# The opening of a two-layer trunk on one core: x first on the link, c spread from two row groups, A and B of the first tiles in steps, idle transposes in a second place, and other orders

## The chip, the cores and the metric

The kernel runs on one core of one Trainium2 chip. The metric is the device time of one launch in microseconds (us). The core has five engines that work side by side: TensorE (PE) for matrix products, VectorE (DVE) and ScalarE (ACT) for elementwise work, GpSimd (POOL), which this kernel leaves alone, and SyncE (SP), which issues most of the loads and stores. Engines wait for one another by semaphores. Each runs its own list of instructions in order, so an instruction that waits holds up all that stand behind it on its engine. Loads and stores run on 16 DMA engines, the link to memory. TensorE writes its sums into PSUM, which has eight banks of 128 x 512 numbers; everything else lies in SBUF, in 128 partitions.

## What is computed

The reference runs `DEPTH` = 2 layers over a residual stream x of 256 rows and 2048 columns. Cut to what matters:

```python
def hybrid_layer(x, c, ...):
    mod = (c @ w_ada + b_ada)[:, None, :]
    shift, scale, gate = jnp.split(mod, 3, axis=-1)
    h = rms_norm(x, g_pre) * (1 + scale) + shift
    z = h @ w_in
    u, g_pool, q, k, v, g_diff = jnp.split(z, splits, axis=-1)
    pool_out = multiscale_pool(u, w_pool, pool_scale) * jax.nn.silu(g_pool)
    q, k = apply_rope(q, cos, sin), apply_rope(k, cos, sin)
    att = rms_norm(diff_attention(q, k, v, lam), subln_g) * (1.0 - lam_init)
    diff_out = att.reshape(B, S, D_DIFF) * jax.nn.silu(g_diff)
    y = jnp.concatenate([pool_out, diff_out], axis=-1) @ w_out
    return x + (1 + gate) * rms_norm(y, g_post)
```

c is one vector of 2048 numbers, `w_ada` is 2048 x 6144, `w_in` 2048 x 6144 and `w_out` 2048 x 2048 in each layer, all in float32. Every weight is used once for 256 rows.

## The kernel before

**Tiles.** The 256 rows are two row tiles of 128 (`st` 0 and 1). The 2048 columns of x are 16 k tiles of 128, taken in pairs (`kp` 0 to 7). `w_in` has 12 column blocks of 512, named by what they hold: U 0 and 1, GP 2 and 3, Q 4 and 5, K 6 and 7, V 8 and 9, GD 10 and 11. A `Unit` is one block with one pair of k tiles: 512 KB of weights. A weight is split into a rounded part (`whi`, a copy on ACT) and a rest (`wlo`, a subtraction on DVE), and h likewise, so that three fast products make one of full precision. Only the first group of units (three blocks with the first pair) is multiplied in float32 directly from the loaded tile (`rawz`), at about twice the time per product, for which no split is needed.

**The vector c.** `w_ada` isn't multiplied on TensorE. It comes transposed, 128 output columns at a time (`nt` 0 to 47: shift, scale and gate, 16 each), in two halves `i` of 1024 (512 KB each). DVE multiplies each half with c, which stands in every partition (`cb`), and adds up along the row (`ada`, one instruction of 128 x 1024, its sum into `mod`). Behind the two halves of shift and scale, `ab` makes A (the shift with its bias) and B (the scale with bias and `g_pre`) of these k tiles by three small operations. c is loaded into one row and spread to 128 partitions by four products with a row of ones (`spread_c`), each copied from PSUM by ACT; the third and fourth copies stand behind the squares of the first row tile.

**h.** `first_squares` sums the squares of x, `rms` makes the norm's factor from them (a sum, a root on ACT, three small operations on DVE), `scaled` scales x, PE transposes it, and ACT applies A and B (`modulated`). `make_h` and `half_h` do this for the first pair in halves by row tile. `half_h` keeps its bank with the transposed x until A and B of both k tiles are made and it has issued `first(0)` and `first(1)`, the rounded parts of h. With `st` 0 it also issues `WARM` = 18 transposes of the identity on PE, whose output nobody reads.

**Banks.** `BANKS` = 4 and `ACCS` = 4. The sums of the first two blocks of the first group lie in the `accs`, those of the third in two of the four `banks` (`prepare`, `wide`; they are named accb in the trace). The other small PSUM work takes from the rest of `banks`.

**Order.** The order on every engine is made by a planner, `Flow`, when the program is built. Each part of the kernel is a `Task` that asks for one instruction after another; the planner keeps an estimate of every engine's time, and at each step gives the turn to the request that can start first, by due times (`due`). `COST`, `MB_US`, `LANDING` and `FIRST` are its prices; `SLACK` is a margin that transposes and small products get on PE behind the estimated end of what they read; `need(u, before)` is the time at which unit u will be reached, less a lead. `RATE` says how many halves of `w_ada` are counted per unit when `plan` lays out the units, and `ORDERS` which column block takes which place in the order in which a layer's blocks end. The first steps of PE's main stream (`steps`) are: the first k tile of three blocks with row tile 0, then with row tile 1, then the second k tile of three blocks with both.

**Loads.** `begin` issues c, the positions and, by `first_loads`, x, the first halves of `w_ada` and the raw weights, all on SP's queue in the order of issue. ACT's queue takes two constants: `consts` (the frequencies and an identity) and `cols` (biases and gains by column).

Of the kernel before, what the change touches and what calls it, by code (L numbers as in the profile page):

```python
# [14 lines left out]
I32 = mybir.dt.int32  # L15
# [8 lines left out]
P = 128  # L24
# [105 lines left out]
class Flow:  # L130
# [9 lines left out]
    TABLE_US = 1.29  # L140
    MB_US, LANDING, FIRST = 0.38, 2.4, 2.2
    COLD = (1.8, 4.0)

    SLACK = 1.5
    NEAR = {"tensor": 0.0, "vector": 0.1, "scalar": 0.1, "gpsimd": 0.1, "sync": 0.0}
# [65 lines left out]
    def next_of(self, k, asks):  # L211

        rows = []
        for t in asks:
            a = t.ask
            if a.dep is None:
                a.dep = self.depends(a)
            us = a.us + self.TABLE_US * bool(a.table and a.table[0] != self.table)
            due = t.due()
            slack = self.SLACK * (k == "tensor" and 0 < due < 1e8)  # L220
            rows.append((due, max(self.now[k], a.dep + slack), us, t))
        rows.sort(key=lambda r: r[:2])
# [28 lines left out]
    def turn(self, key, op, outs, ins, total, table):  # L251
# [7 lines left out]
        a.also, self.cur.also = self.cur.also, []  # L259
        a.names = {r[0] for r in a.outs + a.ins} | {r[0] for _, r in a.also}  # L260
        a.dep, a.f32 = None, key == "tensor" and op == "matmul" and ins[-1].dtype == F32
        if a.dma:
# [142 lines left out]
class Kern:  # L405
# [169 lines left out]
    def run(self):  # L575
# [10 lines left out]
        self.wps, self.G, self.nlam, self.band = [None] * DEPTH, [None] * DEPTH, None, None  # L586
        self.rope_made = False
        self.ada_tiles = {}
# [3 lines left out]
    def begin(self):  # L592
        nc, a, f = self.nc, self.a, self.f
        self.cb = self.const([P, D], "cb")
        nc.sync.dma_start(self.cb[0:1, :], a["c"])
        consts = self.const([P, HALF + P], "consts")
        nc.scalar.dma_start(consts, a["consts"])
        self.invf, self.ident = consts[:, :HALF], consts[:, HALF:]
        self.pos_i = self.const([P, NST], "posi", I32)
        nc.sync.dma_start(self.pos_i, a["positions"])  # L600
        self.cols = self.const([P, DEPTH, 89], "cols")
        nc.scalar.dma_start(self.cols, a["cols"])
        self.x = [self.const([P, D], f"x{st}_") for st in range(NST)]
# [9 lines left out]
        self.root_table()  # L613
        self.arrived, self.squared = [False] * NST, False
        f.spawn(self.first_loads, -95.0)
        f.spawn(self.spread_c, -90.0)
        for st in range(NST):
# [12 lines left out]
        for l in range(DEPTH):  # L630
            f.spawn(lambda l=l: self.load_pool_weights(l))
            for kp in range(8):
                f.spawn(lambda l=l, kp=kp: self.make_h(l, kp), self.need_h(l, kp, 4.0))

    def first_loads(self):
# [12 lines left out]
        tiles = {u: self.big.take([P, 2, NB], "raw", kind="raw") for u in us}  # L648
        x(0)
        for e in self.adas[:4]:  # L650
# [21 lines left out]

# [185 lines left out]
    def ada(self):  # L858

        v = self.nc.vector  # L860
        for e in self.adas:
# [17 lines left out]
    def ab(self, l, k0, k1):  # L879
# [26 lines left out]
    def first_squares(self, st):  # L906
# [6 lines left out]
        if st:  # L913

            f.wait(lambda: self.made[0])
            more = self.big.take([P, D // 2], "junk")
            self.nc.vector.scalar_tensor_tensor(
                more, x[:, c[1]], self.ROOT**2, x[:, c[1]], op0=ALU.mult, op1=ALU.mult, accum_out=ss[:, st, 3:4]
            )
            self.big.give(more)  # L920
# [55 lines left out]
    def half_h(self, l, kp, st, hi, lo, whole):  # L976
# [11 lines left out]
        if whole is not None and not st:  # L988

            d = self.bank()  # L990
            for i in range(self.WARM):
                nc.tensor.transpose(d[:, 0:P], self.ident, self.ident)
            self.banks.give(d)

# [24 lines left out]
        rest(0), rest(1)  # L1019
        self.used_whole(kp)  # L1020

    def used_whole(self, kp):
# [221 lines left out]
    def heads(self, l, hp):  # L1244
# [11 lines left out]
        for h in range(2):  # L1256
# [183 lines left out]
def _constants():  # L1440
    s = np.arange(S)
    band = np.zeros((4, S, S), np.float32)
    for g, w in enumerate(WINDOWS):
# [4 lines left out]
    return {  # L1448
        "consts": np.concatenate([np.broadcast_to(np.array(INV_FREQ, np.float32), (P, HALF)), np.eye(P, dtype=np.float32)], axis=1),
        "band": blocks.transpose(1, 0, 2),  # L1450
# [32 lines left out]
```

## Time and profile before

| | |
|---|---|
| median of three runs | 818.13 us (816.19 to 821.13) |
| the profiled execution | 817.44 us |
| its span, first to last instruction | 815.7 us |
| mean granted TensorE clock | 0.995 |
| read from memory | 242.17 MB, 299 GB/s over the span |
| halves of `w_ada`, 512 KB each | 192 loads |
| raw weights, 512 KB each | 253 loads, and 6 of 256 KB |

How to read the rows: a row of the timeline has its start, its duration, the engine, the operation with the tile that it writes and those it reads, the shapes, and in brackets how long its engine had been idle and what ended that. SPq and ACTq are the queues that issue loads. Every operation has the line L125, since all are issued through one helper; so one goes by the names of the tiles (buffer numbers left out): `adaz` is a half of `w_ada`, `cb` c in all partitions, `psb` a bank, `accc` and `accb` the sums, `halfz` one of many half tiles, `rawz` the raw weights, `whiz` and `wloz` their parts, `hz` those of h, `zz` a result block, `consts` the identity. A float32 product is two records. PE's busy time counts the ends of products that overlap, so that what PE loses is read from its waits and from the starts of its rows.

### The profile page before, as it was taken

What the parts mean: (1) busy time and instruction counts of PE and PEld (TensorE: products, weight loads), DVE (VectorE), ACT (ScalarE), POOL (GpSimd) and SP (SyncE); (2) the same over time, 40 slices, a digit from 0 to 9 for tenths busy, and PEclk for the clock granted to TensorE, in tenths of its full rate; (3) what the DMA queues carried; (4) which work ended last, traced back from release to release, by engine and by line L of the source; (5) the groups of instructions that cost most, each with busy time, mean ns of one, the idle gap of its engine ahead of it and who ended that gap; (6) DMA issues with size and microseconds to landing.
All of it is one profiled execution on the core that took longest, in us unless ns stands there. A gap on an engine that the chain in (4) does not pass through costs nothing. (4 is left out here: it accounts for less than half of the span.)

```text
span 815.7 us, 11813 instructions
## 1 busy us (share of the span) xinstructions
PE 794.2 (97%) x4032; PEld 658.5 (81%) x4032; DVE 697.3 (85%) x1232; ACT 545.8 (67%) x971; POOL 0.2 (0%) x4
## 2 busy tenths in 40 slices
PE   7899999999999999999999999999999999999995
PEld 3588789888997878788888889898898897787884
DVE  7889999998888899899999989878799889877924
ACT  4679998786655586886387557666656467677721
POOL 0000000000000000000000000000000000000000
PEclk9999999999999999999999999999999999999998
DMA  8999998999999877767999889999999895456302
GB/s 344 406 410 408 408 409 284 371 383 372 348 366 334 295 226 239 249 205 251 336 344 358 283 306 384 336 380 334 327 373 395 298 328 187 143 164 211 118 1 103
DMA packets 68382, 245.06 MB, mean 300 GB/s; under 512 B 7745, under 2 KB 8033, under 8 KB 68065
## 3 DMA queue, kind: packets, MB, share of 16 engines
q1 hardware_dynamic: 68034, 244.14, 82.6%
q8 instruction: 31, 0.51, 0.2%
q10 hardware_dynamic: 288, 0.17, 0.1%
q14 instruction: 29, 0.24, 0.1%
HBM read 242.17 MB, written 2.11 MB: 299 GB/s over the span
## 5 line engine op out<-in xcount | busy, mean ns | idle before, releaser
L125 PE MATMUL accc<-whiz,hz 128*128 128x512 f32 x1256 | 395.3, 393 | 1.2 <-ACT accc L125 0.7
L125 ACT CAST whiz<-rawz 128x1024 fp32r<-128x1024 f32 x253 | 260.1, 1052 | 104.6 <-DMA rawz<-in_w_in 66.9
L125 DVE TENSOR_TENSOR wloz<-rawz,whiz 128x1024 fp32r<-128x1024 f32 x253 | 303.5, 1219 | 12.3 <-ACT whiz L125 11.4
L125 PEld LDWEIGHTS accc<-whiz,hz 128*128 128x128 f32 x1256 | 234.7, 188 | 51.9 <-DVE hz L125 1.8
L125 DVE SCALAR_TENSOR_TENSOR adaz<-adaz,cb 128x1024 f32<-128x1024 f32 x192 | 231.2, 1219 | 35.3 <-DMA adaz<-in_w_ada 34.5
L125 PE MATMUL accc<-wloz,hz 128*128 128x512 f32 x628 | 245.5, 391 | 0.9 <-DVE wloz L125 0.9
L125 PE MATMUL accc<-whiz,catz 128*128 128x512 f32 x512 | 165.1, 398 | 1.0 <-ACT zz L125 1.0
L125 PEld LDWEIGHTS accc<-wloz,hz 128*128 128x128 f32 x628 | 118.0, 188 | 25.6 <-DVE wloz L125 1.7
L125 PEld LDWEIGHTS accc<-whiz,catz 128*128 128x128 f32 x512 | 94.6, 188 | 21.1 <-ACT zz L125 1.8
L125 PE MATMUL accc<-wloz,catz 128*128 128x512 f32 x256 | 101.6, 397 | 0.0
L125 ACT COPY accc<-zz 128x512 f32<-128x512 f32 x110 | 65.0, 591 | 29.0 <-DVE halfz L125 19.5
L125 ACT COPY zz<-accc 128x512 f32<-128x512 f32 x121 | 70.1, 585 | 14.4 <-PE accc L125 13.7
L125 PE MATMUL accc<-hz,whiz 128*128 128x256 f32 x512 | 72.1, 283 | 0.0
L125 PEld LDWEIGHTS accc<-hz,whiz 128*128 128x128 f32 x512 | 66.7, 192 | 0.8
L125 PEld LDWEIGHTS accc<-wloz,catz 128*128 128x128 f32 x256 | 48.1, 188 | 10.1 <-issue 0.7
L125 PE MATMUL accc<-hz,wloz 128*128 128x256 f32 x256 | 42.0, 284 | 0.0
L125 PEld LDWEIGHTS accc<-hz,wloz 128*128 128x128 f32 x256 | 35.6, 192 | 0.0
L125 ACT ACTIVATE sqj<-accc 128x512 bf16<-128x512 f32 x16 | 9.5, 597 | 37.9 <-PE accc L125 37.7
L125 PE MATMUL psb<-consts,halfz 128*128 128x128 f32 x176 | 30.5, 276 | 4.5 <-ACT halfz L125 2.4
L125 PEld LDWEIGHTS psb<-consts,halfz 128*128 128x128 f32 x176 | 22.1, 141 | 13.7 <-ACT halfz L125 4.9
L125 DVE TENSOR_TENSOR yz<-accc,Gz 128x512 f32<-128x512 f32 x16 | 10.9, 689 | 24.0 <-ACT sqj L125 23.8
L125 ACT ACTIVATE halfz<-psb,sm 128x128 f32<-128x128 f32 x64 | 26.3, 419 | 1.3 <-DVE sm L125 1.0
(112 smaller groups left out, 515.9 us busy)
## 6 DMA issues: line engine op xcount, KB each, us to landing
adaz<-in_w_ada SPq DMA_DIRECT2D x192, 512.0 KB, 7.2
rawz<-in_w_in SPq DMA_DIRECT2D x189, 512.0 KB, 7.8
rawz<-in_w_out SPq DMA_DIRECT2D x64, 512.0 KB, 4.0
x<-in_x SPq DMA_DIRECT2D x2, 1024.0 KB, 8.0
wpz<-in_w_pool SPq DMA_DIRECT2D x4, 512.0 KB, 6.6
Gz<-gate SPq DMA_DIRECT2D x4, 512.0 KB, 6.7
out<-x SPq DMA_DIRECT2D x8, 256.0 KB, 2.1
rawz<-in_w_in SPq DMA_DIRECT2D x6, 256.0 KB, 9.1
```

Of the source, the lines that this page charges most:

```text
L125: return f(*args, **kw)
```

## The change

- x of the first row tile is the first load on SP's queue. c goes on ACT's queue in two halves, into rows 0 and 64 of a tile, then `consts`, which now holds `cols` too, then the positions.
- `spread_c` works in two steps. Each takes two banks, multiplies 512 numbers out of row 0 and 512 out of row 64, and copies one bank by ACT and the other by DVE.
- The first row tile's squares wait for the spreading; one half is done by DVE (`half_square`), the other by ACT. Its root has the due time 13.0.
- A and B of the first two k tiles of layer 0 are made by `ab_step`: A when its two halves are there, a part of B (`most`) behind the first half of the scale, and B by one operation behind the second.
- `warm(1)` issues 16 transposes of the identity ahead of the second k tile's products of the first group.
- Of the planner's numbers `LANDING`, `SLACK`, two of `RATE`, both `ORDERS` and several leads differ; `FED` is new and is 0.0.

```diff
-    MB_US, LANDING, FIRST = 0.38, 2.4, 2.2
+    MB_US, LANDING, FIRST = 0.38, 2.6, 2.2
-    SLACK = 1.5
+    SLACK = 1.2
+    FED = 0.0
...
-            slack = self.SLACK * (k == "tensor" and 0 < due < 1e8)
+            slack = self.SLACK * (k == "tensor" and 0 < due < 1e8) + self.FED * (a.fed and due > 40)
...
-    WARM = 18
+    WARM = (18, 16)
-    RATE = {(0, 2): 0.82, (1, 2): 0.75, (0, 0): 0.92, (0, 1): 0.9, (1, 0): 0.8, (1, 1): 0.35}
-    ORDERS = [[10, 2, 3, 11, 6, 4, 0, 1, 7, 8, 5, 9], [2, 10, 0, 6, 11, 3, 4, 8, 5, 1, 7, 9]]
+    RATE = {(0, 2): 0.82, (1, 2): 0.85, (0, 0): 0.92, (0, 1): 0.9, (1, 0): 0.8, (1, 1): 0.4}
+    ORDERS = [[10, 2, 3, 4, 6, 0, 11, 1, 7, 8, 5, 9], [2, 10, 0, 6, 8, 3, 11, 4, 5, 1, 7, 9]]
...
     def begin(self):
+        self.x = [self.const([P, D], f"x{st}_") for st in range(NST)]
+        nc.sync.dma_start(self.x[0], a["x"][0:P, :])
+        half = self.big.take([P, D // 2], "c")
+        for i, r in enumerate((0, 64)):
+            nc.scalar.dma_start(half[r : r + 1, :], a["c"][:, i * D // 2 : (i + 1) * D // 2])
+        consts = self.const([P, HALF + P + DEPTH * 89], "consts")
+        nc.scalar.dma_start(consts, a["consts"])
...
+        nc.scalar.dma_start(self.pos_i, a["positions"])
-        nc.sync.dma_start(self.cb[0:1, :], a["c"])
-        nc.sync.dma_start(self.pos_i, a["positions"])
-        nc.scalar.dma_start(self.cols, a["cols"])
-        self.ones = self.const([1, P], "ones")
+        self.ones = self.const([P, P], "ones")
...
-                f.spawn(lambda l=l, kp=kp: self.make_h(l, kp), self.need_h(l, kp, 4.0))
+                f.spawn(lambda l=l, kp=kp: self.make_h(l, kp), self.need_h(l, kp, 3.5))
...
-    def spread_c(self):
-        for j in range(4):
-            b, c = self.bank(), self.cb[:, j * 512 : (j + 1) * 512]
-            nc.tensor.matmul(b, self.ones, c[0:1, :], start=True, stop=True)
-            if j == 2:
-                self.f.wait(lambda: self.squared)
-            nc.scalar.copy(c, b)
-            self.banks.give(b)
+    def spread_c(self, half):
+        for j in range(2):
+            b = self.banks.take([P, NB], "ps", n=2)
+            for i, r in enumerate((0, 64)):
+                nc.tensor.matmul(b[i], self.ones[r : r + 1, :], half[r : r + 1, j * NB : (j + 1) * NB], start=True, stop=True)
+            nc.scalar.copy(self.cb[:, j * NB : (j + 1) * NB], b[0])
+            nc.vector.tensor_copy(self.cb[:, (2 + j) * NB : (3 + j) * NB], b[1])
+            self.banks.give(*b)
+        self.big.give(half)
+        self.spread = True
...
-            if i and 16 <= nt < 32 and (nt % 2 or not l and nt < 18):
+            if not l and nt % 16 < 2 and nt < 32:
+                self.ab_step(l, nt, i)
+            elif i and 16 <= nt < 32 and nt % 2:
                 kt = nt - 16
-                self.ab(l, kt if not l and kt < 2 else kt - 1, kt + 1)
+                self.ab(l, kt - 1, kt + 1)
                 self.made[l] = kt + 1
+    def ab_step(self, l, nt, i):
+        v, kt = self.nc.vector, nt % 16
+        m = lambda j: self.mod[l][:, j, nt : nt + 1]
+        b = self.b1[:, l, nt : nt + 1]
+        if nt < 16 and i:
+            v.scalar_tensor_tensor(self.AB[l][:, 0, kt : kt + 1], m(0), m(1), b, op0=ALU.add, op1=ALU.add)
+        elif nt >= 16 and not i:
+            self.most = self.small([P, 1], "most")
+            v.tensor_tensor(self.most, m(0), b, op=ALU.add)
+        elif nt >= 16:
+            g = self.cols[:, l, 48 + kt : 49 + kt]
+            v.scalar_tensor_tensor(self.AB[l][:, 1, kt : kt + 1], m(1), self.most, g, op0=ALU.add, op1=ALU.mult)
+            self.made[l] = kt + 1
...
     def first_squares(self, st):
...
-            square(0), square(1)
+            f.wait(lambda: self.spread)
+            self.half_square(st), square(0)
             self.squared = True
...
-        self.xr[0][st] = self.rms(ss[:, st, 2:5])
+        self.xr[0][st] = self.rms(ss[:, st, 2:5], None if st else 13.0)
...
+    def warm(self, n):
+        d = self.bank()
+        for i in range(self.WARM[n]):
+            self.nc.tensor.transpose(d[:, 0:P], self.ident, self.ident)
+        self.banks.give(d)
...
     def prepare(self):
-                self.f.due(self.need(self.units[w.at], 4 - st - (1.36 * u.count if w in turn and st else 0)))
+                self.f.due(self.need(self.units[w.at], 4.5 - st - (1.36 * u.count if w in turn and st else 0)))
...
     def products(self):
...
+            if u.group == 1 and n == NST * self.count:
+                self.warm(1)
             self.mm(u, sts, ks)
...
-                    self.f.spawn(lambda g=g: self.pool_group(l, g), self.need_cat(l, g, 8.0))
+                    self.f.spawn(lambda g=g: self.pool_group(l, g), self.need_cat(l, g, 12))
...
-            f.spawn(one, self.need_cat(l, 4 + hp, 20.0 - h))
+            f.spawn(one, self.need_cat(l, 4 + hp, 22 - h))
-        f.due(self.need_cat(l, 4 + hp, 14.0))
+        f.due(self.need_cat(l, 4 + hp, 16))
```

More of the change, by code (lines that the diff above doesn't have):

```diff
@@ L260, in turn @@
         a.names = {r[0] for r in a.outs + a.ins} | {r[0] for _, r in a.also}
+        a.fed = not a.dma and any(r[0].startswith(("ada", "raw")) for r in a.ins)
         a.dep, a.f32 = None, key == "tensor" and op == "matmul" and ins[-1].dtype == F32
@@ L586, in run @@
         self.wps, self.G, self.nlam, self.band = [None] * DEPTH, [None] * DEPTH, None, None
-        self.rope_made = False
+        self.rope_made, self.spread = False, False
         self.ada_tiles = {}
@@ L593, in begin @@
         nc, a, f = self.nc, self.a, self.f
-        self.cb = self.const([P, D], "cb")
-        nc.sync.dma_start(self.cb[0:1, :], a["c"])
[L596 to L599, printed above, removed]
-        nc.sync.dma_start(self.pos_i, a["positions"])
-        self.cols = self.const([P, DEPTH, 89], "cols")
-        nc.scalar.dma_start(self.cols, a["cols"])
-        self.x = [self.const([P, D], f"x{st}_") for st in range(NST)]
+        self.x = [self.const([P, D], f"x{st}_") for st in range(NST)]
[5 more added lines that the diff above has]
+        nc.scalar.dma_start(consts, a["consts"])
+        self.invf, self.ident = consts[:, :HALF], consts[:, HALF : HALF + P]
+        self.cols = consts[:, HALF + P :].rearrange("p (l c) -> p l c", l=DEPTH)
+        self.pos_i = self.const([P, NST], "posi", I32)
+        nc.scalar.dma_start(self.pos_i, a["positions"])
+        self.cb = self.const([P, D], "cb")
         self.mod = [self.const([P, 2, 48], "mod") for l in range(DEPTH)]
@@ L613, in begin @@
         self.root_table()
-        self.arrived, self.squared = [False] * NST, False
+        self.arrived, self.squared = [True, False], False
         f.spawn(self.first_loads, -95.0)
-        f.spawn(self.spread_c, -90.0)
+        f.spawn(lambda: self.spread_c(half), -90.0)
         for st in range(NST):
@@ L648, in first_loads @@
         tiles = {u: self.big.take([P, 2, NB], "raw", kind="raw") for u in us}
-        x(0)
         for e in self.adas[:4]:
@@ L915, in first_squares @@
             f.wait(lambda: self.made[0])
[L916 to L920, printed above, removed]
+            self.half_square(st)
             f.wait(lambda: (0, 0) in self.h_whole)
@@ L927, in first_squares, with half_square @@
         f.due(-80.0 + 75.0 * st)
-        self.xr[0][st] = self.rms(ss[:, st, 2:5])
+        self.xr[0][st] = self.rms(ss[:, st, 2:5], None if st else 13.0)
+    def half_square(self, st):
+        x, c = self.x[st], slice(D // 2, D)
+        more = self.big.take([P, D // 2], "junk")
+        self.nc.vector.scalar_tensor_tensor(
+            more, x[:, c], self.ROOT**2, x[:, c], op0=ALU.mult, op1=ALU.mult, accum_out=self.xss[0][:, st, 3:4]
+        )
+        self.big.give(more)
     def scaled(self, out, x, r):
@@ L988, in half_h @@
         if whole is not None and not st:
[L990 to L993, printed above, removed]
+            self.warm(0)
         def first(i):
@@ L1448, in _constants @@
     return {
-        "consts": np.concatenate([np.broadcast_to(np.array(INV_FREQ, np.float32), (P, HALF)), np.eye(P, dtype=np.float32)], axis=1),
+        "consts": [np.broadcast_to(np.array(INV_FREQ, np.float32), (P, HALF)), np.eye(P, dtype=np.float32)],
         "band": blocks.transpose(1, 0, 2),
@@ L1463 @@
         "positions": i["positions"].reshape(NST, P).T,
-        "cols": np.concatenate([cols(i[k]) for k in ("b_ada", "g_pre", "g_post", "pool_scale", "subln_g")], axis=2),
         "lam": np.stack([i[k] for k in ("lambda_q1", "lambda_k1", "lambda_q2", "lambda_k2")], axis=1).reshape(1, -1),
@@ L1471 @@
     }
+    names = ("b_ada", "g_pre", "g_post", "pool_scale", "subln_g")
+    host["consts"] = np.concatenate(host["consts"] + [np.concatenate([cols(i[k]) for k in names], axis=2).reshape(P, -1)], axis=1)
     host = {k: np.ascontiguousarray(v) for k, v in host.items()}
```

## The prediction

> **What bounds the kernel now.** I read the page's first part, then the windows, then what TensorE (PE) waited for behind the start, then the start row by row. The page's busy shares:
>
> ```profile
> PE 794.2 (97%) x4032; PEld 658.5 (81%) x4032; DVE 697.3 (85%) x1232; ACT 545.8 (67%) x971; POOL 0.2 (0%) x4
> ```
>
> Busy time by stretch of the span; behind the engines stand the granted TensorE clock, the DMA share and GB/s:
>
> ```profile
> 15.00:31.25 16.25, 13.31 (x33) 5.66 (x32) 13.42 (x34) 11.49 (x22) 0.00 (x0) 0.89 1.03 407
> 31.25:60.00 28.75, 28.75 (x152) 24.55 (x151) 25.80 (x39) 21.41 (x34) 0.00 (x0) 1.00 1.03 409
> 60.00:100.00 40.00, 38.94 (x194) 32.27 (x193) 38.99 (x57) 38.49 (x59) 0.00 (x0) 1.00 1.03 408
> ```
>
> All waits of PE between 31 us and 808 us (sum, times, longest):
>
> ```profile
> PE psb L125 <- DVE halfz L125: 2.1, 2, 1.2
> PE accc L125 <- ACT zz L125: 1.0, 2, 0.7
> PE accc L125 <- DVE wloz L125: 0.9, 1, 0.9
> PE accc L125 <- ACT accc L125: 0.7, 1, 0.7
> PE accc L125 <- DVE hz L125: 0.6, 2, 0.4
> PE psb L125 <- ACT halfz L125: 0.4, 1, 0.4
> ```
>
> From 31.25 us, the end of the first group, to 808 us PE waits 5.7 us in all. A change that adds no work to PE there can win at most these 5.7 us and what it takes off the first 31 us. Between 60 and 100 us VectorE (DVE) is busy 38.99 of 40 us, ScalarE (ACT) 38.49, and the link is full (1.03, 408 GB/s): a gain at the start must pass three engines that have no room.
>
> **The start, step by step.** The rows that carry it:
>
> ```profile
> 0.73 0.35 SPq L125 DMA_DIRECT2D cb<-in_c  x1
> ...
> 1.54 0.42 SPq L125 DMA_DIRECT2D x<-in_x  x1
> ...
> 2.68 7.16 PE L125 MATMUL psb<-cb,ones 1*128 1x512 f32 x8 [2.68 <-DMA cb<-in_c]
> ...
> 6.95 1.06 ACT L125 ACTIVATE junkz<-x 128x1024 bf16<-128x1024 f32 x1
> ...
> 9.88 0.59 ACT L125 COPY cb<-psb 128x512 f32<-128x512 f32 x1 [0.27 <-PE psb L125]
> ...
> 8.57 1.23 DVE L125 SCALAR_TENSOR_TENSOR adaz<-adaz,cb 128x1024 f32<-128x1024 f32 x1
> ...
> 11.13 1.22 DVE L125 SCALAR_TENSOR_TENSOR adaz<-adaz,cb 128x1024 f32<-128x1024 f32 x1
> ...
> 12.29 3.48 PE L125 MATMUL psb<-consts 128*128 128x128 f32 x18
> ...
> 15.33 0.46 ACT L125 ACTIVATE halfz<-psb,AB 128x128 f32<-128x128 f32 x1 [3.58 <-DVE AB L125]
> 15.41 1.23 DVE L125 SCALAR_TENSOR_TENSOR junkz<-x 128x1024 f32<-128x1024 f32 x1
> ...
> 22.33 1.23 DVE L125 SCALAR_TENSOR_TENSOR adaz<-adaz,cb 128x1024 f32<-128x1024 f32 x1 [0.40 <-DMA adaz<-in_w_ada]
> ...
> 23.60 0.16 DVE L125 TENSOR_TENSOR AB<-mod 128x2 f32<-128x2 f32 x1
> 23.80 0.17 DVE L125 TENSOR_TENSOR AB<-AB,b 128x2 f32<-128x2 f32 x1
> 24.00 0.16 DVE L125 TENSOR_TENSOR AB<-AB,cols 128x1 f32<-128x1 f32 x1
> ...
> 24.19 0.81 ACT L125 ACTIVATE halfz<-psb,AB 128x128 f32<-128x128 f32 x2 [2.90 <-DVE AB L125]
> 24.70 5.40 PE L125 MATMUL accc<-rawz,halfz 128*128 128x512 f32 x8 [2.32 <-ACT halfz L125]
> 24.89 1.50 ACT L125 ACTIVATE hz<-psb,AB 128x128 fp32r<-128x128 f32 x4
> ```
>
> On DVE stand four ada products of c ahead of the first scaled tile (15.33 us) and four more ahead of the second (24.19 us). The eighth starts at 22.33 us on the landing of its tile, so the second k tile waits for the link.
>
> **Part 1, x first.** SP issued c and the positions ahead of x; now x goes at 0.73 us instead of 1.54 us. Everything behind it on SP's queue, with the link full, comes 1.54 - 0.73 = 0.81 us earlier. ACT now issues four small loads instead of two before its table load; nothing there is late, as its first work is the copy of PE's first pair. **-0.81 us for what waits on a load**; bounds -0.81 and 0 (if the small loads of ACT take the place).
>
> **Part 2, c from two row groups.** Before: eight matmul records, 7.16 us, 0.895 each, four ACT copies, c whole at 9.88 + 0.59 = 10.47 us. Whether two row groups run side by side is seen at the heads, where pairs stand in rows 0 to 63 and 64 to 127:
>
> ```profile
> L125 PE MATMUL psb<-halfz,wpz 128*128 128x256 f32 x64 | 14.9, 380 | 0.0
> ...
> L125 PE MATMUL psb<-zz,zz 64*128 64x256 f32 x64 | 9.6, 377 | 0.0
> ```
>
> Same count, width and mean, but 9.6 us of union instead of 14.9: they overlap. So a pair costs two records, 1.79 us. The second pair needs the same two banks (two of the four hold the third block's sums), so it waits for the copies of the first. The second half of c is issued 0.4 us behind the first: 3.1 + 1.79 + 0.59 (a copy, by ACT's row) = 5.5, and again + 2.38 = 7.9 us: 2.6 us earlier. Without overlap it is 3.1 + 2 x (3.58 + 0.59) = 11.4 us, 0.9 later. But DVE now does one half of x's squares too, and it waits for c's spreading; behind it on DVE stand the four products. From 7.9: square 1.23, four products of 1.22, 4.9; four norm steps, ab_step's two early operations and its last, seven at 0.17 to 0.2 with their gaps (the AB rows stand 0.2 apart), 1.4: 15.4 us. The scaled tile started at 15.33 us. **First product: 0**; bounds -2.6 (if the square finds room elsewhere) and +0.9. The 2.6 us go into DVE's square and into the first ada product, which at 8.57 us ran beside the spreading before.
>
> **Part 3, AB in steps.** Behind the last product of the tile stood three operations, 23.60 to 24.16 us; now one, as long as this kind:
>
> ```profile
> L125 DVE SCALAR_TENSOR_TENSOR rh<-ry,rs 128x1 f32<-128x1 f32 x8 | 1.8, 219 | 0.3
> ```
>
> 0.56 - 0.22 = 0.34, with a gap **-0.33 us**. The second k tile is ready at 24.70 - 0.81 - 0.33 = 23.56 us.
>
> **Part 4, sixteen transposes.** They are meant for PE's 2.32 us gap, after which the clock was low:
>
> ```profile
> 15.84:18.50 2.66, 2.66 (x6) 1.06 (x6) 0.00 (x0) 0.00 (x0) 1.00 1.04 414
> ...
> 24.70:31.25 6.55, 6.55 (x12) 2.79 (x12) 2.86 (x3) 4.30 (x5) 0.74 1.02 409
> ```
>
> (The products of the first group alone.) Twelve at the pace of the six are 5.32 us, so the low clock costs 6.55 - 5.32 = 1.23 us. But `warm(1)` takes a bank. At that place two of four hold sums and two hold the transposed x of both row tiles, which `half_h` gives back only behind `first(0), first(1)`, the hz rows, the second of which ends (24.89 + half of 1.50, less 24.70) 0.94 us after the products used to start. The products stand behind the transposes on PE, and behind the products the copies of their sums on ACT and DVE. So: **+0.94 us** of waiting (0 if a bank is free), then sixteen transposes on the path. One costs 0.11 us at full clock:
>
> ```profile
> 678.79 0.44 PE psb L125 x4
> ```
>
> and 0.19 in the early row of 18: **+1.76 us** to 3.1. What they save is -1.23 us, if the clock stays up. The clock's rows speak against it: PE's work before it ended at 24.70 - 2.32 = 22.38 us, the transposes start at 23.56 + 0.94 = 24.50: 2.1 us idle, and at 2.32 us the clock fell.
>
> The Trainium skill, page "TensorE: Matmul & The Clock Gate", section "What's actually happening", has it that the clock falls after an idle window of about 3.4 us of a free-running counter. Read as idle for 3.4 us in a row the gate would not have fallen here; the measured 0.74 says it did. By that reading the group would end at +0.3 us, by the rows at +1.6 us.
>
> End of the first group against 31.25 us: -0.81 - 0.33 + 0.94 + 1.76 = +1.56 us with the low clock paid again (my value, by the gap of 2.32 us, the nearest row), +0.33 with it saved; -2.37 if a bank is free and the transposes lie in the gap (-0.81 - 0.33 - 1.23).
>
> **Part 5, the stage that follows.** PE's first stop behind it, and the two of the rotary stage with DVE's rows:
>
> ```profile
> 80.36 0.50 PE L125 MATMUL accc<-wloz,hz 128*128 128x512 f32 x1 [0.87 <-DVE wloz L125]
> ```
>
> ```profile
> 261.97 0.66 PE L125 MATMUL psb<-consts,halfz 128*128 128x128 f32 x4 [1.23 <-DVE halfz L125]
> ...
> 265.29 0.66 PE L125 MATMUL psb<-consts,halfz 128*128 128x128 f32 x4 [0.82 <-DVE halfz L125]
> ```
>
> ```profile
> 256.62 1.23 DVE L125 SCALAR_TENSOR_TENSOR adaz<-adaz,cb 128x1024 f32<-128x1024 f32 x1 [0.39 <-DMA adaz<-in_w_ada]
> ...
> 260.08 1.23 DVE L125 SCALAR_TENSOR_TENSOR adaz<-adaz,cb 128x1024 f32<-128x1024 f32 x1 [0.96 <-DMA adaz<-in_w_ada]
> ```
>
> A PE that is 1.56 us late meets at 80.36 us a wait of 0.87 us (0.2 more at the shorter one on hz, by the table of waits): 0.5 us stay. A PE that is 2.37 us early waits longer there, since DVE has no room from 60 to 100 us and starts its share 0.8 us earlier at best. **At 100 us: +0.5**, bounds -2.4 and +1.6.
>
> **Part 6, the planner's numbers.** `RATE[1, 2]` and `RATE[1, 1]` move nothing: in `plan` they only take gate tiles (nt of 32 and more) from a list, which set no `kp_at`, and the order of the ada loads is a copy made before. `FED` is 0.0. `LANDING` 2.6, `SLACK` 1.2, the new leads and `ORDERS` reorder the queues. The trace of before doesn't show the new order. Bounds: -4.6 (every wait of the table behind 100 us gone) and, from the rotary rows, 2.1 + 2 x 0.3 = +2.7 for each rotary block that meets the late DVE with 0.3 us less slack. DVE stood 0.39 + 0.96 us on loads that came later than planned; 0.2 us more `LANDING` goes against that. I take **-1.3**, one such wait gone, near the row.
>
> **Sum.** 817.44 us (span 815.7 and 1.7 around it) + 0.5 - 1.3 = **816.6 us**. The median of before, 818.13 us, is 0.7 above the profiled execution; I don't add it.
>
> **The rivals.** 0.5% is 4.1 us, about what a measurement of this kernel can tell from no change; the bounds of the classes are 814.0 and 822.2 us.
>
> A. Forecast, 816.6 us: 0.44.
>
> B. The start's gain gets through: a bank is free, or DVE, with the rotary tables put off, keeps pace, and the new order takes two thirds of the 5.7 us: 817.44 - 2.37 - 3.8 = 811.3 us. For it: the waits are few and each is a matter of order. Against: 38.99 of 40. 0.27.
>
> C. Slower: the rotary wait spreads. With `SLACK` 1.2 PE meets DVE's last rotary operation, when that is over 1.2 us behind plan. One of eight Q and K blocks pays now; two more: 816.6 + 1.3 + 2 x 2.7 = 823.3 us. Against: seven blocks pay nothing today. 0.14.
>
> D. c comes late. It lies now on ACT's queue beside a megabyte of x:
>
> ```profile
> cols<-in_cols ACTq DMA_DIRECT2D x1, 89.0 KB, 2.8
> consts<-in_consts ACTq DMA_DIRECT2D x1, 80.0 KB, 2.1
> ```
>
> If it lands with x (x's first square began at 6.95 us, so 6.1), c is whole at 6.1 + 2 x 2.38 = 10.9 us, the first product 3 us later, the group some 3 us; a third of it is taken up at 80 us: 818.6 us. The Trainium skill, page "DMA: Bandwidth & Descriptors", section "Issuing engines are not separate DMA queues", says that both queues run on the same engines and interleave, which would let a small load pass between x's packets. 0.06.
>
> E. It does nothing: the start is absorbed and the order is as good as the old: 817.4 us. 0.09.
>
> Faster by over 0.5% is B, 0.27; slower is C, 0.14; the rest, 0.59, within. The range reaches from below B to short of C's 823.3: 810.5 to 822.5; A's own is 814 to 819.5.
>
> **What would show it.** x at 0.73 us on SP, and the ada wait of 22.33 us at 21.5 us. c's copies over by 7.9 us, in pairs of ACT and DVE; the first scaled tile near 15.3 us. One operation between the eighth product and the scaled tile. The sixteen transposes behind two hz rows and not in the gap; were they in the gap, part 4 is wrong and B likely. The clock between 25 and 33 us. The wait at 80 us shorter. The rotary waits near 262 us. Wrong above all: a sum of PE's waits behind 31 us that leaves 3 to 8 us.

## The result, and the profile after

The changed kernel takes 821.18 us (median of 11 runs, 820.06 to 824.58) against 816.02 us for the kernel before beside it (11 runs, 813.34 to 821.13): ratio 1.0064, 95% interval 1.0042 to 1.0087. It is slower by 5.2 us, where 816.6 us and no change were forecast. Its profiled execution is one of the two longest of the eleven: 824.58 us, span 822.8 us, clock 0.994; that of before took 817.44 us.

The start of the changed kernel, from its timeline (start, duration, engine, operation, and in brackets the idle time and what ended it):

```profile
0.73 0.39 SPq L125 DMA_DIRECT2D x<-in_x  x1
...
1.54 0.40 ACTq L125 DMA_DIRECT2D consts<-in_consts  x1
1.97 0.88 ACTq L125 DMA_DIRECT2D posi<-in_positions  x1
...
6.16 2.11 PE L125 MATMUL psb<-cz,ones 1*128 1x512 f32 x4 [0.63 <-DMA cz<-in_c]
...
9.39 0.18 DVE L125 COPY b<-consts 128x32 f32<-128x32 f32 x1 [8.14 <-DMA consts<-in_consts]
...
10.89 0.17 DVE L125 CAST posf<-posi 128x2 f32<-128x2 int32 x1 [1.10 <-DMA posi<-in_positions]
...
12.71 0.69 DVE L125 COPY cb<-psb 128x512 f32<-128x512 f32 x1
...
13.45 2.07 PE L125 MATMUL psb<-cz,ones 1*128 1x512 f32 x2 [5.18 <-DVE cb L125]
15.55 0.69 DVE L125 COPY cb<-psb 128x512 f32<-128x512 f32 x1 [1.25 <-PE psb L125]
16.16 1.22 DVE L125 SCALAR_TENSOR_TENSOR junkz<-x 128x1024 f32<-128x1024 f32 x1
...
20.36 0.51 ACT L125 ACTIVATE halfz<-x,ry 128x256 f32<-128x256 f32 x1 [1.52 <-DVE ry L125]
...
21.40 3.58 PE L125 MATMUL psb<-consts 128*128 128x128 f32 x18
...
23.16 0.46 ACT L125 ACTIVATE halfz<-psb,AB 128x128 f32<-128x128 f32 x1 [2.29 <-DVE AB L125]
...
24.82 1.88 PE L125 MATMUL accc<-rawz,halfz 128*128 128x512 f32 x4
...
29.78 1.22 DVE L125 SCALAR_TENSOR_TENSOR adaz<-adaz,cb 128x1024 f32<-128x1024 f32 x1
...
31.04 0.22 DVE L125 SCALAR_TENSOR_TENSOR AB<-mod,most,consts 128x1 f32<-128x1 f32 x1
...
31.29 0.81 ACT L125 ACTIVATE halfz<-psb,AB 128x128 f32<-128x128 f32 x2 [3.02 <-DVE AB L125]
...
31.99 1.50 ACT L125 ACTIVATE hz<-psb,AB 128x128 fp32r<-128x128 f32 x4
...
32.85 1.97 PE L125 MATMUL psb<-consts 128*128 128x128 f32 x16 [1.68 <-ACT hz L125]
...
34.65 3.60 PE L125 MATMUL accc<-rawz,halfz 128*128 128x512 f32 x8
...
39.41 0.80 PE L125 MATMUL accc<-whiz,hz 128*128 128x512 f32 x1
```

Read it from the end. The first group ends at 39.41 us instead of 31.25. Its first product starts at 24.82 us instead of 15.84: that is 9.0 us, all of the loss, of which 0.8 us is won back inside the group. The last piece of c is copied at 15.55 to 16.24 us, where 7.9 us was forecast. PE could not make that piece before 13.45 us, since the bank was held by the DVE copy of 12.71 us, and that copy stands on DVE behind table work that waited 8.14 us for `consts` and 1.10 us more for the positions. These two are the small loads that the change put behind c on ACT's queue. From issue to landing (last number, us), first the changed kernel, then the kernel before, whose `consts` row of 2.1 us is shown above:

```profile
consts<-in_consts ACTq DMA_DIRECT2D x1, 169.0 KB, 7.8
...
posi<-in_positions ACTq DMA_DIRECT2D x1, 1.0 KB, 8.9
```

```profile
posi<-in_positions SPq DMA_DIRECT2D x1, 1.0 KB, 2.0
```

Behind the start, PE's waits from 45 to 808 us in the changed kernel (sum, times, longest):

```profile
PE psb L125 <- ACT zz L125: 2.0, 1, 2.0
PE accc L125 <- DVE hz L125: 0.4, 1, 0.4
PE accc L125 <- DVE wloz L125: 0.4, 1, 0.4
PE psb L125 <- DVE halfz L125: 0.3, 1, 0.3
```

They sum to 3.1 us; before they were 5.7. So the group's end, +8.2 us, and the later waits, -2.6 us, give +5.6 us, beside +5.2 in the medians. The two rotary waits of before near 262 us (2.1 us on DVE's halfz) are gone; the 0.3 us on the same pair stands behind 640 us, and one new wait of 2.0 us has come at 639 us. Behind that new wait the granted clock was 0.50 for 3 us, which adds an estimated 1.6 us (PE's busy time of each microsecond, times what its clock lacks to 1). With it the profiled executions are accounted for: 8.2 - 2.6 + 1.6 = 7.2 us, and they lie 7.1 us apart.

### The profile page after: what moved, and what is told of

Same layout as the page of the kernel before. It is cut to its first block, busy times and chain, and to the rows that moved or that the text cites. A ratio compares the mean times of both kernels' runs of the same rounds, so it can differ in the third digit from the quotient of the medians.

```text
span 822.8 us, 11841 instructions
## 1 busy us (share of the span) xinstructions
PE 793.6 (96%) x4048; PEld 660.0 (80%) x4048; DVE 695.8 (85%) x1228; ACT 548.7 (67%) x975; POOL 0.2 (0%) x4
## 3 DMA queue, kind: packets, MB, share of 16 engines
HBM read 242.17 MB, written 2.11 MB: 297 GB/s over the span
## 5 line engine op out<-in xcount | busy, mean ns | idle before, releaser
L125 ACT COPY zz<-accc 128x512 f32<-128x512 f32 x124 | 71.8, 586 | 19.2 <-PE accc L125 18.3
```

Of the source, the lines that this page charges most:

```text
L125: return f(*args, **kw)
```

## The experiments

For the changed kernel and the eleven others the table has the start of the first product behind the first group (its end) and the sum of PE's waits from 45 to 808 us. "Sum" is the first plus the second, less 31.25 + 5.7 of before. "Clock" is the estimate of what a low clock cost in the same stretch, worked out as above; it was nothing before. "Profiled" is the time of the profiled run less the 817.44 us of before. "Median" is the difference of the medians to the kernel before on the same chip.

| kernel | group's end | later waits | sum | clock | profiled | median | ratio, 95% interval |
|---|---|---|---|---|---|---|---|
| changed kernel | 39.41 | 3.1 | +5.6 | +1.6 | +7.1 | +5.2 | 1.0064 (1.0042 to 1.0087) |
| c_ahead | 33.68 | 8.6 | +5.3 | +1.5 | +8.1 | +3.3 | 1.0036 (1.0004 to 1.0068) |
| tables_later | 34.89 | 7.2 | +5.1 | +2.2 | +7.9 | +7.7 | 1.0093 (1.0059 to 1.0128) |
| numbers_only | 30.80 | 2.0 | -4.2 | 0 | -4.0 | -4.6 | 0.9948 (0.9924 to 0.9971) |
| start_only | 40.79 | 4.4 | +8.2 | 0 | +10.1 | +9.1 | 1.0111 (1.0076 to 1.0147) |
| c_tables | 34.46 | 10.1 | +7.6 | +2.7 | +11.0 | +9.4 | 1.0114 (1.0083 to 1.0146) |
| c_tables_no_warm | 30.22 | 3.6 | -3.1 | 0 | -2.5 | -4.0 | 0.9952 (0.9935 to 0.9970) |
| after_no_warm | 36.06 | 2.3 | +1.4 | 0 | +1.7 | +2.1 | 1.0022 (1.0002 to 1.0043) |
| numbers_steps | 29.29 | 2.7 | -5.0 | 0 | -4.7 | -4.0 | 0.9962 (0.9945 to 0.9979) |
| steps_warm | 33.13 | 3.4 | -0.4 | +1.7 | +1.3 | -0.6 | 0.9993 (0.9969 to 1.0017) |
| squares_act_early | 28.89 | 3.7 | -4.4 | 0 | -3.0 | +0.3 | 0.9993 (0.9969 to 1.0017) |
| squares_halves | 29.93 | 4.7 | -2.3 | +1.7 | +0.5 | +1.8 | 1.0016 (0.9988 to 1.0044) |

Within one execution the account holds: sum and clock together are within 2 us of the profiled time in all twelve rows. So the time is the start, a few single waits and the low clock behind some of them. The median stands for other executions too, and sum and median agree within 2.6 us in ten rows; the last two miss by 4 to 5 us and come at the end.

A group's end has a spread of its own. Before, numbers_only, numbers_steps and steps_warm issue the same first loads in the same order, and the first row tile of x landed 5.3, 7.3, 5.1 and 6.9 us behind its issue. Differences of 1 to 2 us between two groups' ends are read with that in mind.

The times of c_ahead, tables_later, start_only, c_tables and the last two lie outside of what the theory behind them gave; each is said below.

**c_ahead.** The changed kernel with c's two halves on SP ahead of x, and only `consts` and the positions on ACT.

```diff
-        nc.sync.dma_start(self.x[0], a["x"][0:P, :])
-            nc.scalar.dma_start(half[r : r + 1, :], a["c"][:, i * D // 2 : (i + 1) * D // 2])
+            nc.sync.dma_start(half[r : r + 1, :], a["c"][:, i * D // 2 : (i + 1) * D // 2])
+        nc.sync.dma_start(self.x[0], a["x"][0:P, :])
```

> The changed kernel, with the two halves of c issued on SP's queue ahead of x; the constants and the positions stay on ACT's queue, alone there. Theory L (the small loads land late beside x and the w_ada tiles, and DVE's list, in which work on constants and positions stands ahead of a copy of c, waits for them): the small loads land within 3.5 us, c is whole by 8.5 us instead of 16.2, the first product starts at 15 to 17 us instead of 24.8, the first group ends near 32 us instead of 39.4, and the time is 815 to 818 us, 3 to 6 below the changed kernel. Theory O (the new orders, leads and margin cost the time in later stages): 820 to 822 us, as changed, though the start is earlier.

The loads, and DVE's first and second copy of c with the first product:

```profile
consts<-in_consts ACTq DMA_DIRECT2D x1, 169.0 KB, 2.4
...
posi<-in_positions ACTq DMA_DIRECT2D x1, 1.0 KB, 3.5
```

```profile
6.98 0.68 DVE L125 COPY cb<-psb 128x512 f32<-128x512 f32 x1
...
9.83 0.69 DVE L125 COPY cb<-psb 128x512 f32<-128x512 f32 x1 [1.25 <-PE psb L125]
...
18.97 1.88 PE L125 MATMUL accc<-rawz,halfz 128*128 128x512 f32 x4
```

The small loads land in 2.4 and 3.5 us, and the group ends 5.7 us sooner. `consts` and the positions are on ACT's queue in both kernels; what differs is that they, and c, are now issued ahead of x. So the place behind x is the first cause. c is whole at 10.5 us, still not at 7.9: DVE's copy of 6.98 us stands behind the table work. The time, 821.47 us, isn't the 815 to 818 of Theory L but lies within Theory O, an earlier start and later stages that cost as much; numbers_only below, which is faster with the same numbers, shows that the numbers by themselves don't cost this. Of the 5.7 us the medians keep 1.9 (+3.3 against +5.2), and the profiled run nothing: its later waits are 8.6 us against 3.1, with one of 4.5 us at 640 us, where the changed kernel waits 2.0. That run, 825.58 us, is one of the longest of twelve (817.38 to 825.70 us), so the others may have less of it.

**tables_later.** The changed kernel, with the columns and the rotary tables (`columns`, `rope_tables`) put behind the spreading; the loads as in the change.

```diff
     def columns(self):
+        self.f.wait(lambda: self.spread)
...
     def rope_tables(self):
+        self.f.wait(lambda: self.spread)
```

> The changed kernel, with the work on the columns of constants and the rotary tables held back until c is spread, so that DVE's copies of c stand first in its list; the loads stay as changed. Theory L with the order on DVE as its larger part: c is whole near 11.6 us, the first product at 18.5 to 20.5 us, time 817 to 819.5 us. If the late landing alone were the cause (c's own second half at 6.2 us), the first product would be near 24 us still and the time 821. Theory O: 820 to 822 us.

DVE's copies of c stand at 8.07 and 10.92 us instead of 12.71 and 15.55, and the group ends 4.5 us sooner, though the loads are where the change has them. So late loads cost because work that needs them stood ahead of c in DVE's list. c is whole at 11.6 us, as expected, and the first product starts at 20.91 us. The time, 825.89 us, misses the 817 to 819.5: a wait of 4.4 us at 304 us, with a clock of 0.50 behind it, takes the gain away, and the median is higher than the changed kernel's.

**numbers_only and start_only.** The change cut in two: the kernel before with only the new `LANDING`, `SLACK`, `ORDERS` and leads; and the changed kernel with these put back.

```diff
-    SLACK = 1.5
+    SLACK = 1.2
...
-                f.spawn(lambda l=l, kp=kp: self.make_h(l, kp), self.need_h(l, kp, 4.0))
+                f.spawn(lambda l=l, kp=kp: self.make_h(l, kp), self.need_h(l, kp, 3.5))
```

> The kernel before with the new LANDING, SLACK, ORDERS and leads alone; the start as before. Theory L: as fast as before or up to 2.5 us faster (813.5 to 816.5 us), since the changed kernel's waits of PE behind the first group are 3.1 us against 5.7. Theory O: 3 to 6 us slower than before, 819 to 822 us.

> The changed kernel with LANDING, SLACK, ORDERS and leads of before; the start as changed. Theory L: at least as slow as the changed kernel, 821 to 824 us, first product near 24.8 us. Theory O: 815 to 817 us.

The halves have opposite signs: the numbers by themselves are worth 4.6 us, the rewritten start costs 9.1 us, and its 827.28 us lie above the 821 to 824 of Theory L. PE's later waits in numbers_only, to be read against the six rows of before:

```profile
PE accc L125 <- DVE hz L125: 0.7, 2, 0.4
PE accc L125 <- ACT zz L125: 0.5, 1, 0.5
PE accc L125 <- DVE wloz L125: 0.5, 1, 0.5
PE psb L125 <- DVE halfz L125: 0.3, 1, 0.3
```

2.1 us on DVE's halfz have become 0.3, and the sum 2.0: 3.7 of the 4.6 us. The group's end, 30.80 us, says little of the numbers: x landed 2.0 us later than in the profile of before and the first product started 1.8 us later, but the second k tile ran at full clock, 4.85 us (25.95 to 30.80) where before took 6.55 at 0.74.

**c_tables, c_tables_no_warm, after_no_warm.** The two repairs of the start together; the same without `warm(1)`; and the changed kernel without `warm(1)`.

```diff
-            if u.group == 1 and n == NST * self.count:
-                self.warm(1)
```

> The changed kernel with both edits: c ahead of x on SP's queue, and the work on constants held back until c is spread. If the start's loss is the late small loads plus DVE's list, the two together bring c whole to 8 to 8.5 us (10.5 with the loads alone moved, 16.2 as changed), the first product to 16 to 17 us (19.0 and 24.8) and the first group's end to 32 to 32.8 us (33.7 and 39.4; 31.25 before). If the split squares on DVE were the larger part, the first product stays near 19 us. The time: 813 to 820 us, since a later wait of up to 5 us comes and goes with the order.

> As the kernel with both edits, but without the sixteen idle transposes and the bank they take. If they stand on the path, as forecast, the products of the second k tile start right behind the scaled tiles and the group ends 1 to 2.5 us earlier, at 30 to 31.5 us, even if the clock falls (1.2 us of it). If the transposes earn their time by the clock, it ends no earlier, at 32.4 us or later.

> The changed kernel without the sixteen idle transposes alone. On the path: the group ends at 36.5 to 38.3 us instead of 39.4, and the time is 818 to 820.5 us; no gain if DVE's load from 60 to 100 us takes it up again, 821. If the clock's fall costs more than the transposes: 39.5 us or later, 821 to 822.5 us.

The second k tile of c_tables, and below it that of c_tables_no_warm:

```profile
24.67 0.81 ACT L125 ACTIVATE halfz<-psb,AB 128x128 f32<-128x128 f32 x2 [3.76 <-DVE AB L125]
25.37 1.50 ACT L125 ACTIVATE hz<-psb,AB 128x128 fp32r<-128x128 f32 x4
26.23 2.85 PE L125 MATMUL psb<-consts 128*128 128x128 f32 x16 [2.42 <-ACT hz L125]
28.87 4.44 PE L125 MATMUL accc<-rawz,halfz 128*128 128x512 f32 x8
```

```profile
24.86 0.81 ACT L125 ACTIVATE halfz<-psb,AB 128x128 f32<-128x128 f32 x2 [3.80 <-DVE AB L125]
25.37 3.70 PE L125 MATMUL accc<-rawz,halfz 128*128 128x512 f32 x8 [1.41 <-ACT halfz L125]
```

The modulated tiles are ready within 0.2 us of one another. With the transposes the products start 4.20 us behind them, without 0.51 us. c_tables ends its group at 34.46 us and not at 32 to 32.8, since the clock fell there: 0.67 over the transposes and 0.85 over what follows. The group's end moves by 4.2 us here and by 3.4 us in after_no_warm, where 1.0 of it is a tile that was ready sooner. The median falls by 13.4 us, more than the start: the later waits drop from 10.1 to 3.6 us too, as another start gives another order, and the low clock behind them (2.7 us) is gone.

**numbers_steps and steps_warm.** The new numbers with `ab_step`, the start otherwise as before; then the same with the sixteen transposes.

```diff
-            if i and 16 <= nt < 32 and (nt % 2 or not l and nt < 18):
+            if not l and nt % 16 < 2 and nt < 32:
+                self.ab_step(l, nt, i)
+            elif i and 16 <= nt < 32 and nt % 2:
```

> The kernel before with the new LANDING, SLACK, ORDERS and leads (as in the run of the numbers alone) and, of the start, A and B in steps alone. The operations behind the eighth product fall from three to one, so the second k tile is scaled 0.3 to 0.4 us earlier than with the numbers alone; the time is that of the numbers alone, 813 to 814.5 us. If the steps, which stand between products on DVE, delay the products, the first product is 0.2 us later and the time 814 to 815 us.

> numbers_steps (new numbers and A and B in steps, the start of before otherwise; first group's end at 29.29 us, 813.0 us, 0.9962 of before) with the sixteen transposes alone added ahead of the second k tile. The start isn't late here, so this is their price by itself. Theory (they wait for a bank behind the hz rows and lie on the path): PE waits on ACT's hz, the transposes run 2.0 us or, with the clock low after a gap of 2.3 us, up to 2.9; the group ends 3.3 to 4.3 us later, 32.6 to 33.6 us, and the time is 3 to 5 us longer, 816 to 818 us, ratio 1.000 to 1.002; if the planner then leaves the single long waits of c_tables behind 45 us as well (7.7 us against 2.7 in numbers_steps), up to 823. Rival (the transposes are worth their time, because they keep the clock up, and what they cost was a matter of the late start): the group ends by 30 us and the time stays at 813, ratio 0.996.

numbers_steps takes 813.0 us and beats both kernels, as do numbers_only and c_tables_no_warm; their intervals overlap, so the runs do not rank the three. steps_warm shows the price of the transposes where nothing is late:

```profile
25.02 0.81 ACT L125 ACTIVATE halfz<-psb,AB 128x128 f32<-128x128 f32 x2 [1.69 <-DVE AB L125]
25.72 1.50 ACT L125 ACTIVATE hz<-psb,AB 128x128 fp32r<-128x128 f32 x4
26.58 1.97 PE L125 MATMUL psb<-consts 128*128 128x128 f32 x16 [2.16 <-ACT hz L125]
28.38 3.60 PE L125 MATMUL accc<-rawz,halfz 128*128 128x512 f32 x8
```

From the tile to the products it is 3.36 us, in numbers_steps 0.51 (23.93 to 24.44 us): 2.85 us for the wait and the transposes. The other 1.0 us of the group's later end comes from a first product 1.2 us later. That is no price of the transposes: DVE has the same list up to there, and its first product with c waits for a load that landed later, below in numbers_steps and then in steps_warm.

```profile
8.53 1.23 DVE L125 SCALAR_TENSOR_TENSOR adaz<-adaz,cb 128x1024 f32<-128x1024 f32 x1 [0.67 <-DMA adaz<-in_w_ada]
```

```profile
9.98 1.23 DVE L125 SCALAR_TENSOR_TENSOR adaz<-adaz,cb 128x1024 f32<-128x1024 f32 x1 [1.84 <-DMA adaz<-in_w_ada]
```

Against the kernel before, the median goes from -4.0 to -0.6 us.

**squares_act_early and squares_halves.** Both put c ahead, put the rotary tables behind the spreading and drop `warm(1)`; the first row tile's squares no longer wait for c. In the first both halves are on ACT, in the second one stays on DVE.

```diff
-            f.wait(lambda: self.spread)
-            self.half_square(st), square(0)
+            square(0), square(1)
```

> The changed kernel with c ahead of x on SP, the rotary tables behind the spreading, no second transposes, and the first row tile's squares as before: both halves on ACT, not waiting for c, the root as early as it can be; the products with c wait for the whole of c. Against c_tables_no_warm (first product 17.38 us, group end 30.22, 813.0 us) it takes the norm of x from behind c and the half square (1.22 us) from DVE. Theory (the change's own second loss is that the norm of x stands behind c: the factor ry came at 12.89 us in c_tables against 11.05 before, and the eighteen transposes ahead of the first product 1.84 us later): ry by 11 us, first product near 15.8, the group's end 28.7 to 29.3 us; the time by the group's end and PE's waits behind 45 us (3.6 us there) 1 to 1.5 us shorter, 811.5 to 812; up to 3 us either way if the planner's order moves a late wait. Rival (the list of the products with c alone sets the start): the first product moves, the group's end stays at 30.2 and the time at 813.

> The same, but one half of the first row tile's squares stays on DVE, as in the changed kernel, only without the wait for c. It tells whether the wait or the place on DVE was what cost. Theory (the wait): DVE has nothing to do from 6 to 8 us in c_tables_no_warm, x lands by 7 us, so the half square fits ahead of c's second copy; ry by 10.5 to 11 us, first product near 15.5, group end 28.7 to 29.3, time 811 to 812 with the waits unchanged. Rival (the place on DVE): the half square holds up c's second copy by up to 1.2 us and all products with c behind it; group end 29.9 to 30.4, time 813.

From squares_act_early:

```profile
11.32 0.51 ACT L125 ACTIVATE halfz<-x,ry 128x256 f32<-128x256 f32 x1 [1.63 <-DVE ry L125]
...
16.20 2.21 PE L125 MATMUL accc<-rawz,halfz 128*128 128x512 f32 x4
...
28.89 0.80 PE L125 MATMUL accc<-whiz,hz 128*128 128x512 f32 x1
```

The start goes as expected: x is scaled at 11.32 us, against 13.08 in c_tables, and the group's end is the earliest of all. With one half on DVE x is scaled at 12.57 us and the group ends at 29.93 us, as the rival has it, but not by the rival's path. The products with c aren't held up: the first starts at 9.49 us against 9.54 in squares_act_early, and B of the first k tile is made at 15.08 against 15.20. What is later is the square of the second row tile on DVE, 16.39 against 15.35 us, behind rotary table work and a later landing of x (ACT waits for it until 16.39). These 1.04 us are the whole difference of the groups' ends. What a half square on DVE costs by itself is not shown.

The times miss both expectations: 817.05 and 818.47 us. The runs of squares_act_early lie between 813.56 and 819.63 us, and its profiled run, 814.47 us, is one of the shortest, so its waits are not those of the median run. The two profiles show one thing that changes between executions. Both kernels wait for DVE's wloz at the same place, equally long, and then run on; first squares_act_early, then squares_halves, each with the stretch behind it (PE's busy time and records, granted clock, DMA share, GB/s):

```profile
422.61 0.50 PE L125 MATMUL accc<-wloz,hz 128*128 128x512 f32 x1 [1.56 <-DVE wloz L125]
...
424.00:427.50 3.50, 3.50 (x17) 1.00 0.71 280
```

```profile
422.79 0.50 PE L125 MATMUL accc<-wloz,hz 128*128 128x512 f32 x1 [1.55 <-DVE wloz L125]
...
424.00:427.50 3.50, 3.50 (x11) 0.52 0.89 352
```

One clock fell to 0.52 and the other didn't. In squares_act_early the mean clock goes with the time: 0.998 in the four shortest runs (813.56 to 815.56 us), 0.994 to 0.997 in the eight others (816.87 to 819.63 us). That the eight lose their time behind such waits is likely, but no trace of them was kept, so it is not shown.

## Why the prediction was wrong, step by step

**Part 1 and Part 2 failed: "nothing there is late, as its first work is the copy of PE's first pair".** That looked at ACT, which issues the four small loads. Who reads two of them is DVE, and on DVE's list their work stands ahead of c's copy. The parts took c whole at 7.9 us and the first product at 0 (bounds -2.6 and +0.9); it was 16.2 us and +9.0. The table work that stands ahead of DVE's copies was put at nothing: with the loads on time c is whole at 10.5 us (c_ahead), and at 8.7 us once that work stands behind it too (c_tables). Rival D had the place right, and c's second half was used at 6.16 us, where D had 6.1. But D priced this landing alone, 3 us, at a chance of 0.06, and saw neither `consts` and the positions nor DVE's list; in all it cost 8.2 us at the group's end. The Trainium skill, page "DMA: Bandwidth & Descriptors", section "Issuing engines are not separate DMA queues", says that loads of different issuers interleave; the reading made of it, that a small load passes, is not borne out by the 7.8 and 8.9 us here. That x alone on the first place wins 0.81 us was not tried by itself; the issue rows show x at 0.73 us.

Two row groups do run side by side, as forecast: four records took 2.11 us (at 6.16 us), two alone 2.07 us (at 13.45). That gain was real and lay on no path.

A second part of the same step was wrong. It set the first product by the scaled tile at 15.33 us. In the changed kernel that tile is ready at 23.16 + 0.46 = 23.62 us, and the product starts at 24.82, behind the eighteen transposes, which follow the scaled x. The norm of x stands behind c and the half square there, and so does the first product.

**Part 3 held**: one operation (31.04 us) where three stood. From the start of the eighth product to the scaled tile it is 1.51 us (29.78 to 31.29) against 1.86 before (22.33 to 24.19): 0.35 us won, 0.33 forecast. At the group's end it can't be seen: numbers_steps ends its group 1.5 us sooner than numbers_only, but its first product is as much earlier, its x having landed 2.2 us sooner.

**Part 4 was right on the path and wrong on the clock.** The transposes wait for the bank behind the hz rows (1.68 us idle, at 32.85 us) and lie on the path. Forecast 0.94 + 1.76 = 2.70 us, measured 2.85 us in steps_warm. The sum lets the products behind them pay the low clock again, after 2.1 us idle. It was 1.68 us idle and a clock of 1.00, and the rest of the group took 4.76 us (34.65 to 39.41) against 6.55 before. These 1.8 us are why 0.8 us is won back inside the group in spite of the transposes. But it isn't shown that the transposes earned them: without them the products of numbers_steps, numbers_only and c_tables_no_warm started after gaps of 1.4 to 1.6 us and ran at full clock too.

**Part 5 was right in that nearly all goes through.** Of the two waits that it names, 0.87 us is 0.40 and 0.19 is gone: 0.7 us, where 1.07 was taken. How much of this is PE's lateness is open, since numbers_only, which isn't late, has 0.46 us in place of 0.87.

**Part 6 was mis-sized.** -1.3 us was taken; numbers_only shows -4.6 us, the end of the bounds. Not one rotary wait fell but both, and of the other waits half (3.6 to 1.7 us). In the changed kernel the same numbers are worth 3.9 us (start_only +9.1, changed kernel +5.2). So the two errors have opposite signs, and it is by luck that the median still lies inside the range; the start alone, 827.28 us in start_only, is outside of it.

## What to carry to other kernels

When a load is moved to another queue or behind another load, look for who reads it and what stands behind that reader in its engine's list; the issuing engine's own first work says nothing. Where a planner writes the order, cut a change into its start and its numbers before judging it: here -4.6 and +9.1 us lay in one change. Work that is meant to fill a gap needs a free buffer in that gap; otherwise it begins when the gap is over. And set a profile's waits against the time of the profiled execution, not against the median of others.

## What the runs showed of the hardware

**Small loads behind large ones on another queue.** 1 KB took 8.9 us to land when it was issued at 1.97 us, behind x and beside four halves of `w_ada` on SP's queue, against 3.5 us (c_ahead) and 2.0 us (before) when it was issued ahead of x.

**The clock after a gap.** The rows of start_only:

```profile
32.55 2.46 PE L125 MATMUL psb<-consts 128*128 128x128 f32 x16 [1.90 <-ACT hz L125]
34.80 4.83 PE L125 MATMUL accc<-rawz,halfz 128*128 128x512 f32 x8
```

After idle times of 1.90 (start_only), 2.32 (before) and 2.42 us (c_tables) the eight records of the second k tile took 4.4 to 5.4 us; after 1.68 (changed kernel) and 2.16 us (steps_warm) they took 3.60. After 1.55 us in squares_halves the clock fell, after 1.56 us at the same place in squares_act_early it did not. So the length of the gap alone does not decide. The Trainium skill, page "TensorE: Matmul & The Clock Gate", section "What's actually happening", has a window of about 3.4 us that runs freely, so that the moment of a change depends on the phase. The phase fits 1.90 against 2.16 us and 1.55 against 1.56; that a whole idle window of 3.4 us is needed does not fit these rows.

**Single waits.** One planned order against another made or removed single waits of PE of 2 to 4.5 us far behind the change (4.4 us at 305 us in c_tables, 4.5 us at 640 us in c_ahead). They are as large as the gains at the start. The five waits of 2.0 us and more behind 45 us (changed kernel, c_ahead, tables_later, c_tables, steps_warm) were each followed by 3 to 5 us at a clock of 0.50, which adds 1.5 to 2.7 us by the estimate above; of the shorter ones only that of 1.55 us in squares_halves was (1.7 us).
